# A two-layer decoder trunk: order of TensorE work around four hand-overs, and the memory norm one group earlier

## The chip, the cores and the metric

The kernel runs on one core of a Trainium2 chip. The metric is the device time of one execution in microseconds (us). Before the change it is 2344.69 us, the median of 3 runs (2342.08 to 2345.27). The core's engines are TensorE (PE: matrix multiplications and transposes, PEld its weight loads), VectorE (DVE), ScalarE (ACT), GpSimd (POOL) and SyncE (SP), whose queue issues the loads. Each engine works through its own instructions in a fixed order.

## What is computed

The reference runs a residual stream `x` of 256 rows by 2048 columns through two layers, in float32.

```python
mem_h = rms_norm(mem, mem_norm)
for i in range(DEPTH):                      # 2 layers
    h = rms_norm(x, attn_norm[i])
    if i % N_MIXERS == 0:                   # layer 0: differential attention, 16 heads, causal
        x = x + diff_attention(h, ...)
    else:                                   # layer 1: latent attention, 16 heads, causal
        x = x + mla_attention(h, ...)
    x = x + memory_cross_attention(rms_norm(x, cross_norm[i]), mem_h, ...)   # 4 heads, 256 memory rows
    x = x + sq_relu_mlp(rms_norm(x, mlp_norm[i]), ...)                       # 2048 -> 8192 -> 2048
return rms_norm(x, final_norm)
```

In the latent attention the queries come from a normed 512-wide latent row `c_q`, the keys and values from another, `c_kv`. Each head's query has a part of 128 columns and a rotated part of 64; the rotated key is shared by all heads.

## The kernel before

**Precision.** Every product is made of three passes over rounded halves: an operand is cast to a high part on ACT (`hi`) and the rest is subtracted on DVE (`lo`), and PE sums hi x hi, hi x lo and lo x hi.

**Weights.** `plan` lists the weight pieces in the order of their use, each 512 rows by 512 columns (1 MB). `split_weights` (L84) loads one into one of 3 `raw` tiles, casts its halves on ACT (L98) and subtracts on DVE (L99) into `whi` and `wlo` (4 buffers of half a piece each). `take` (L114) keeps three pieces traced ahead. All loads go through one queue, SP, in the order in which the program issues them (`load`, L75).

**Activations.** They stand transposed in units of 512 columns (`unit`, 10 buffers), with `hi` and `lo` parts for both row tiles (t = 0 and 1, 128 rows each). `matmul_chunk` (L123) multiplies a list of units with the next weight pieces into two PSUM banks, one for each row tile: for each unit 24 matmuls (4 slices of 128 rows, 2 row tiles, 3 passes). The banks come from a pool of four (`ps_mm`, tag `mm`, L53); a second pool of four (`ps_ax`) serves the attention's scores and outputs. `heads_T` (L270) takes a bank on to the next unit: ACT copies it out with a scale (`evacuate`, L250, into one of 3 `ev` tiles), PE transposes four blocks back into the same bank (`transpose4`, L184), and ACT and DVE split it (`split`, L172, lines 176 and 177). Only then is the bank free.

**Residual.** `Stream.feed` (L233) does this for a chunk of the residual when the next norm's input is made: `add_residual` (L247, DVE) adds the bank to `x`, PE transposes the new columns into the same bank, DVE scales them by the norm's gains into a tile `xg` (2 buffers, L181), the split follows, and ACT sums the squares (L205). The row scale itself is applied after the next multiplication.

**Attention.** Both attentions go in four groups of four heads (`attention`, L592). `project(gi)` makes a group's queries, keys and values; `attend(gi)` its softmax and outputs; `project_group` multiplies the group's output `o` into the residual. In program order a turn `gi` holds `attend(gi)`, the output product of group `gi - 1`, `project(gi + 1)` and `mid(gi)`. In the last turn the output product also lays out the transposed memory (`given_unit(memT, c, G_MEM)`, L190, four units, each of which takes a `raw` tile); `mem_keys` follows and then the last group's output product. `mem_norm` (L539), called by `mid`, loads the memory's rows in eight pieces of 256 KB into tiles of the tag `xg` (`memrow`, L543) and sums their squares on ACT.

**Latent group.** `project_latent` (L743) multiplies the rotated queries first into two banks `pr` (L745); POOL rotates them (`rope`, L255, six operations for each row tile, after an ACT copy). The other queries follow (L751, `heads_T` L753), then the keys' chunk (L754), the transposes of the rotated queries back into `pr` (L757) with their split, the keys' `heads_T` (L762) and the values (L763). In the first group `shared_key` (L733) also rotates the shared key, whose tiles `kr` are of the tag `xg`, copies it (L737) and transposes it (L740). The latents' own transposes are scaled into `xg` tiles as well (L707).

**Cross attention.** `attend4` (L328) weighs the memory's values in `weighted` (L359): for each head and each block of 128 memory rows three passes, and for each pair of heads a copy out of the bank (L379, L380). Its values are computed just before (`mem_values`, lines 281 and 282).

**What sets the order.** The code above gives the dependencies and, through its order, the priorities. The order on each engine is fixed when the program is built: a planner goes through the program on its own estimate of times, and on each engine takes the earliest instruction in program order that it holds to be ready (`schedule_with_timeline_sim=True`, L882). Tiles of one tag are given out in the order of their first use in the program. Loads keep program order. `tc.issue_after(ins)` adds an order without a wait: what is traced inside stands behind `ins` on its engine.

Of the kernel before, what the change touches and what calls it, by code (L numbers as in the profile page):

```python
# [17 lines left out]
P = 128  # L18
# [3 lines left out]
CH = 512  # L22
# [17 lines left out]
def trunk(ctx, tc, x, xT, mem, memT, positions, gcols, gfinal, lam_vecs, consts, W, out):  # L40
# [17 lines left out]
    def nm(s):  # L58
        serial[0] += 1
        return f"{s}_{serial[0]}"  # L60
# [48 lines left out]
            ready.append(split_weights(W[name][i, :, : 4 * width], width))  # L109

    taken = [0]
    hooks = {}

    def take():  # L114
        fill()
        got = ready.pop(0)
        fill()
        taken[0] += 1
        if taken[0] in hooks:
            hooks[taken[0]]()  # L120
        return got

    def matmul_chunk(acts, width=CH, turns=False):  # L123

        ps = [bank("mm") for _ in range(NT)]
        n = len(acts)

        def part(u, h, hi, lo, t):
            o = ps[t][:, :width]
            a = acts[u]  # L130
            for k in range(2):
                kk = 2 * h + k
# [6 lines left out]
                nc.tensor.matmul(o, ah, wh, start=first, stop=False)  # L139
                nc.tensor.matmul(o, ah, wl, start=False, stop=False)  # L140
                nc.tensor.matmul(o, al, wh, start=False, stop=last)  # L141

        for u in range(n - 2 if turns else n):
            for h, (hi, lo) in enumerate(take()):
                for t in range(NT):
                    part(u, h, hi, lo, t)
        if turns:
            parts = [(u, h, *w) for u in (n - 2, n - 1) for h, w in enumerate(take())]
            for t in range(NT):
                for p in parts:  # L150
                    part(*p, t)
        return ps
# [72 lines left out]
    class Stream:  # L225


        def __init__(self, gcol):
            self.gcol = gcol
            self.units = {}  # L230
            self.ss = [small.tile([P, 4], F32, tag="ss", name=nm("ss")) for _ in range(NT)]

        def feed(self, c, t, ps):  # L233
# [4 lines left out]
            split(self.units[c], t, scaled(pt, g[:, self.gcol + 4 * c : self.gcol + 4 * c + 4]))  # L238
            sum_squares(self.ss[t][:, c : c + 1], xc)

        def done(self):
            self.rstd = [row_norm(self.ss[t], D)[:, 0:1] for t in range(NT)]
            return [self.units[c] for c in range(4)]

    def add_residual(t, c, ps):
        xc = xs[t][:, c * CH : (c + 1) * CH]
# [37 lines left out]
    def val(v, half, kb, lo, n):  # L284
        return v[:, half, 2 * kb : 2 * kb + 2, :].rearrange("p a b -> p (a b)")[:, lo : lo + n]
# [42 lines left out]
    def attend4(score_pairs, v, dst, causal):  # L328


        pTs = [work.tile([P, 2, 2, 2, S], F32R, tag="pT", name=nm("pT")) for _ in range(2)]

        def probs(t, heads, nk):
            sb = bank()
            scores(sb, [score_pairs(h, nk) for h in heads], nk, t, causal)
            pr, rs = softmax(sb, len(heads))
            nc.vector.tensor_tensor(
                pr.rearrange("p (h k) -> p h k", k=nk), pr.rearrange("p (h k) -> p h k", k=nk),
                rs[:, : len(heads)].unsqueeze(2).broadcast_to([P, len(heads), nk]), ALU.mult,
            )  # L340
            pt = transpose4(pr, sb)
            nb = nk // P
            for p in range(heads[0] // 2, heads[-1] // 2 + 1):
                at = (2 * p - heads[0]) * nb
                src = pt[:, at : at + 2 * nb].rearrange("p (h b) q -> p h b q", b=nb)
                hi = pTs[p][:, 0, :, :nb, t * P : (t + 1) * P]
                nc.scalar.copy(hi, src)
                nc.vector.tensor_tensor(pTs[p][:, 1, :, :nb, t * P : (t + 1) * P], src, f32(hi), ALU.subtract)

        if causal:  # L350
            probs(0, range(4), P)
        for p in range(2):
            for t in range(1 if causal else 0, NT):
                probs(t, range(2 * p, 2 * p + 2), S)
        if callable(v):
            v = v()
        pos_ = [bank() for _ in range(2)]

        def weighted(p, i, kb):  # L359
            q = slice(kb * P if causal else 0, S)  # L360
            o = pos_[p][:, i * S : (i + 1) * S][:, q]
            col = (2 * p + i) * P
            mm3(
                o, val(v, 0, kb, col, P), val(v, 1, kb, col, P),
                pTs[p][:, 0, i, kb, q], pTs[p][:, 1, i, kb, q],
                kb == 0 and (causal or i == 0), kb == 1 and (causal or i == 1),
            )

        if not causal:
            for h in range(4):  # L370
                weighted(h // 2, h % 2, 0)
        for p in range(2):
            po = pos_[p]
            for i in range(2):
                for kb in (0, 1) if causal else (1,):
                    weighted(p, i, kb)
# [102 lines left out]
    acts = []  # L479
# [93 lines left out]
    def project_out(acts_o, gcol):  # L573
        nxt = Stream(gcol)
        for c in range(4):
            ps = matmul_chunk(acts_o)
            for t in range(NT):
                add_residual(t, c, ps[t])
                nxt.feed(c, t, ps[t])
        return nxt  # L580

    def project_group(o, nxt=None, each=None):
        for c in range(4):
            ps = matmul_chunk([o])
            if each:
                each(c)
            for t in range(NT):
                add_residual(t, c, ps[t])
                if nxt:
                    nxt.feed(c, t, ps[t])  # L590

    def attention(project, attend, mid, gcol):  # L592

# [29 lines left out]
    def mlp(l, norm, gnext):  # L623
        a = norm.done()
        rstd = keep2(norm.rstd, 1.0, "r1")
        hid = {}

        def up(b):
            hid[b] = []
            for c in range(2):  # L630
                dst = unit()
                ps = matmul_chunk(a)
                for t in range(NT):
                    r = work.tile([P, CH], F32, tag="ev", name=nm("ev"), bufs=3)
# [20 lines left out]
        down(7, nxt.feed)  # L655
        return nxt


# [5 lines left out]
    def project_diff(gi):  # L664
# [15 lines left out]
    norm, m, mk = attention(  # L680
        project_diff,
        lambda h, o: attend_diff(*h, o, coef, gsub),
        lambda gi: mem_norm() if gi == 2 else None,
        G_CROSS,
    )
    norm = cross(0, norm, m, mk)
# [56 lines left out]
    def project_latent(gi):  # L743
        qr, q, k, v = half_unit(), unit(), unit(), unit()
        pr = matmul_chunk([cq], 256)  # L745
        turned = []
        for t in range(NT):
            e = evacuate(pr[t][:, :256], rq[t])
            rope(e[:, :256].rearrange("p (h d) -> p h d", h=4), cos[:, t, hd:], sin[:, t, hd:], 4, hm)
            turned.append(e)  # L750
        ps = matmul_chunk([cq])  # L751
        for t in range(NT):
            heads_T(ps[t], t, rq[t], q)  # L753
        ps = matmul_chunk([ckv])  # L754
        for t in range(NT):
            for i in range(2):
                nc.tensor.transpose(pr[t][:, i * P : (i + 1) * P], turned[t][:, i * P : (i + 1) * P], ident)  # L757
# [135 lines left out]
```

## Time and profile before

| | us |
|---|---|
| median of 3 runs | 2344.69 (2342.08 to 2345.27) |
| the profiled execution | 2345.17 |
| its span, first to last instruction | 2343.4 |
| PE busy | 2305.9 (98%) |
| DVE, ACT, POOL busy | 1343.3, 1127.8, 186.2 |
| mean granted TensorE clock | 0.994 of full speed |
| read from HBM | 421.48 MB, 181 GB/s over the span |

A row of the timeline gives start, duration, engine, line of the kernel, operation, tiles (out<-in, with buffer numbers left out), a count, and in brackets the idle time before it and what ended that. The durations of matmuls overlap, since they are pipelined: the distance of two starts is what one costs. A row of waits gives the waiting engine and line, what it waited for, the total, the number of waits and the longest. A row of the chain of waits gives start, duration and what the chain passed through. A row of stretches gives the stretch, its length, the busy time and instructions of PE, PEld, DVE, ACT and POOL, the granted TensorE clock, the share of the DMA engines and GB/s.

### The profile page before, as it was taken

The numbers are of one execution on the slowest core, as the hardware profiler recorded it, in microseconds if no ns is written. First come the engines' busy times: TensorE is split into PE (matmuls) and PEld (weight loads), VectorE is DVE, ScalarE is ACT, GpSimd is POOL, SyncE is SP. The second block draws the span as 40 slices with busy tenths as digits, with TensorE's granted clock in tenths as the row PEclk, the third lists the DMA queues.
The fourth block names the chain that finished last, engine by engine and source line by source line (L and its number), as shares of the span: only waits on it lengthen the run. The fifth ranks groups of instructions, "written<-read, shape, count | busy, mean of one in ns | idle before, by whom it ended". The sixth has DMA issues, their size and how long they took to land.

```text
span 2343.4 us, 27471 instructions
## 1 busy us (share of the span) xinstructions
PE 2305.9 (98%) x10860; PEld 1922.8 (82%) x10860; DVE 1343.3 (57%) x1566; ACT 1127.8 (48%) x1539; POOL 186.2 (8%) x258
## 2 busy tenths in 40 slices
PE   8999999999999999999999999999999999999998
PEld 6888887888888888888889788888888888888886
DVE  5565657675545555555566666777455555554554
ACT  6544446554444444444445555555444444444444
POOL 1111010000000000000000211000100000000001
PEclk9999999999999999999999999999999999999999
DMA  7545556545555555555555343544555555555554
GB/s 277 173 170 171 173 187 208 178 141 184 191 186 197 181 196 184 193 185 193 185 178 179 131 136 135 198 162 162 180 195 182 198 181 195 187 190 183 195 188 153
DMA packets 64354, 425.37 MB, mean 182 GB/s; under 512 B 7392, under 2 KB 7520, under 8 KB 15328
## 3 DMA queue, kind: packets, MB, share of 16 engines
q1 hardware_dynamic: 64224, 423.61, 53.1%
q8 instruction: 85, 1.39, 0.2%
q14 instruction: 45, 0.37, 0.0%
HBM read 421.48 MB, written 2.10 MB: 181 GB/s over the span
## 4 chain that ended last, share of the span: by engine, by line
PE 94%; DMA 2%; ACT 1%; DVE 1%; POOL 1%; issue 1%; SPq 0%; ACTq 0%; POOLq 0%
PE mm L140 29%; PE mm L139 29%; PE mm L141 29%; PE mm L187 3%; PE ax L157 1%; PE ax L155 1%; PE ax L156 1%; DVE wlo L99 1%; DMA raw<-in_da_wqkv_dram 1%; ACT whi L98 1%; DMA raw<-in_ca_wkv_dram 1%; DMA memrow<-in_mem_dram 0%; PE ax L187 0%; DMA x<-in_x_dram 0%; ACT junk L205 0%
## 5 line engine op out<-in xcount | busy, mean ns | idle before, releaser
L99 DVE TENSOR_TENSOR wlo<-raw,whi 128x1024 fp32r<-128x1024 f32 (+2 forms) x794 | 960.5, 1211 | 848.7 <-ACT whi L98 846.3
L98 ACT CAST whi<-raw 128x1024 fp32r<-128x1024 f32 (+2 forms) x794 | 823.9, 1039 | 947.9 <-PE mm L141 900.8
L139 PE MATMUL mm<-whi,unit 128*128 128x512 f32 (+2 forms) x3168 | 1228.3, 389 | 7.8 <-ACT whi L98 5.3
L140 PE MATMUL mm<-wlo,unit 128*128 128x512 f32 (+2 forms) x3168 | 1230.8, 389 | 1.9 <-DVE wlo L99 1.9
L141 PE MATMUL mm<-whi,unit 128*128 128x512 f32 (+2 forms) x3168 | 1231.0, 390 | 0.0
L139 PEld LDWEIGHTS mm<-whi,unit 128*128 128x128 f32 x3168 | 596.9, 189 | 125.5 <-ACT whi L98 7.2
L140 PEld LDWEIGHTS mm<-wlo,unit 128*128 128x128 f32 x3168 | 596.9, 188 | 122.0 <-DVE wlo L99 4.4
L141 PEld LDWEIGHTS mm<-whi,unit 128*128 128x128 f32 x3168 | 596.8, 188 | 115.4
L636 POOL TENSOR_TENSOR ev<-ev 128x512 f32<-128x512 f32 x64 | 81.3, 1271 | 1163.6 <-ACT ev L635 1162.3
L247 DVE TENSOR_TENSOR x<-x,mm 128x512 f32<-128x512 f32 x208 | 135.5, 680 | 14.0 <-PE mm L141 13.5
L176 ACT CAST unit<-mm 128x512 fp32r<-128x512 f32 x104 | 61.0, 587 | 94.7 <-PE mm L187 94.6
L177 DVE TENSOR_TENSOR unit<-mm,unit 128x512 fp32r<-128x512 f32 x104 | 71.2, 687 | 53.7 <-ACT unit L176 53.7
L211 POOL TENSOR_TENSOR rs<-rs,mhalf 128x1 f32<-128x1 f32 (+1 forms) x28 | 19.5, 695 | 669.8 <-DVE rs L210 633.0
L187 PE MATMUL mm<-const,ev 128*128 128x128 f32 x416 | 62.3, 272 | 0.0
L187 PEld LDWEIGHTS mm<-const,ev 128*128 128x128 f32 x416 | 51.3, 140 | 12.3 <-ACT ev L252 0.2
L635 ACT ACTIVATE ev<-mm,r 128x512 f32<-128x512 f32 x64 | 43.8, 685 | 11.5 <-PE mm L141 11.5
L205 ACT ACTIVATE junk<-x 128x512 bf16<-128x512 f32 x56 | 35.2, 629 | 27.1 <-DVE x L247 26.2
L295 ACT ACTIVATE p<-ax,nmax 128x256 f32<-128x256 f32 (+1 forms) x80 | 33.5, 428 | 25.7 <-DVE nmax L293 25.5
L176 ACT CAST unit<-xg 128x512 fp32r<-128x512 f32 x52 | 31.5, 619 | 19.5 <-DVE xg L181 19.5
L177 DVE TENSOR_TENSOR unit<-xg,unit 128x512 fp32r<-128x512 f32 x52 | 34.8, 684 | 0.3
L263 POOL TENSOR_TENSOR rope<-ev,cos 128x64 f32<-128x64 f32 (+1 forms) x24 | 14.5, 603 | 241.7 <-ACT ev L252 240.8
L181 DVE TENSOR_TENSOR xg<-mm,g 128x512 f32<-128x512 f32 x44 | 29.4, 683 | 6.1 <-PE mm L187 4.3
(140 smaller groups left out, 754.0 us busy)
## 6 DMA issues: line engine op xcount, KB each, us to landing
raw<-in_mlp_wup_dram SPq DMA_DIRECT2D x128, 1024.0 KB, 5.0
raw<-in_mlp_wdown_dram SPq DMA_DIRECT2D x128, 1024.0 KB, 4.9
raw<-in_da_wqkv_dram SPq DMA_DIRECT2D x47, 1024.0 KB, 4.8
raw<-in_da_wo_dram SPq DMA_DIRECT2D x16, 1024.0 KB, 4.9
raw<-in_ca_wkv_dram SPq DMA_DIRECT2D x16, 1024.0 KB, 5.0
raw<-in_mla_wo_dram SPq DMA_DIRECT2D x16, 1024.0 KB, 5.0
raw<-in_ca_wq_dram SPq DMA_DIRECT2D x8, 1024.0 KB, 5.0
raw<-in_ca_wo_dram SPq DMA_DIRECT2D x8, 1024.0 KB, 4.9
```

What stands on the lines that cost most here:

```text
L98: nc.scalar.copy(hi, r)
L99: nc.vector.tensor_tensor(lo, r, f32(hi), ALU.subtract)
L139: nc.tensor.matmul(o, ah, wh, start=first, stop=False)
L140: nc.tensor.matmul(o, ah, wl, start=False, stop=False)
L141: nc.tensor.matmul(o, al, wh, start=False, stop=last)
L176: nc.scalar.copy(hi, src)
L177: nc.vector.tensor_tensor(dst[:, 1, :n, t * P : (t + 1) * P], src, f32(hi), ALU.subtract)
L187: nc.tensor.transpose(pt[:, k * P : (k + 1) * P], src[:, k * P : (k + 1) * P], ident)
L205: nc.scalar.activation(junk[:, : src.shape[1]], src, AF.Square, accum_out=acc)
L247: nc.vector.tensor_tensor(xc, xc, ps, ALU.add)
L635: nc.scalar.activation(r, ps[t], AF.Relu, scale=rstd[t])
L636: nc.gpsimd.tensor_tensor(r, r, r, ALU.mult)
```

## The change

Four edits:

1. **Rotated queries.** The four transposes of L757 are put behind the last matmul of the keys' chunk on PE (`behind(latest[0])`; `latest` holds the matmul that `matmul_chunk` traced last).
2. **Last residual chunk.** Where a norm's input is made, the fourth chunk (c == 3) is held: `hold` sums the squares at once, and `last_unit`, called by the next `matmul_chunk` ahead of its second unit, traces the transposes, the scaling and the split behind the last matmul of the first unit. This is so at five places: the output products that end both attentions and both cross attentions, and the last down product of the first MLP.
3. **Cross attention.** The order of the value passes: the passes of the second memory block that use the values' `hi` part go first for all four heads, and those that use the `lo` part last.
4. **Memory norm.** `mem_norm` is called in turn 1 in place of turn 2, behind the projection of the third group.

```diff
+    latest = [None]
+    def behind(mm):
+        return tc.issue_after(mm.ins)
...
-                nc.tensor.matmul(o, al, wh, start=False, stop=last)
+                latest[0] = nc.tensor.matmul(o, al, wh, start=False, stop=last)
         for u in range(n - 2 if turns else n):
+            if u == 1 and callable(acts[-1]):
+                acts[-1] = acts[-1]()
...
+        def hold(self, c, t, ps):
+            sum_squares(self.ss[t][:, c : c + 1], xs[t][:, c * CH : (c + 1) * CH])
+            self.held.append((c, t, ps))
+        def last_unit(self):
+            after = latest[0]
+            for c, t, ps in self.held:
+                with behind(after):
+                    pt = transpose4(xs[t][:, c * CH : (c + 1) * CH], ps)
+                if c not in self.units:
+                    self.units[c] = unit()
+                split(self.units[c], t, scaled(pt, g[:, self.gcol + 4 * c : self.gcol + 4 * c + 4]))
+            self.held = []
+            return self.units[c]
         def done(self):
-            return [self.units[c] for c in range(4)]
+            return [self.units[c] if c in self.units else self.last_unit for c in range(4)]
...
-        def weighted(p, i, kb):
+        def weighted(p, i, kb, passes, first, last):
-            mm3(...)
+            for j, (sv, sp) in enumerate(passes):
+                nc.tensor.matmul(
+                    o, val(v, sv, kb, (2 * p + i) * P, P), pTs[p][:, sp, i, kb, q],
+                    start=first and j == 0, stop=last and j == len(passes) - 1,
+                )
+        PASSES = ((0, 0), (0, 1), (1, 0))
         if not causal:
-            for h in range(4):
-                weighted(h // 2, h % 2, 0)
+            for kb, passes in ((0, PASSES), (1, PASSES[:2]), (1, PASSES[2:])):
+                for p in range(2):
+                    for i in range(2):
+                        weighted(p, i, kb, passes, kb == 0 and i == 0, passes == PASSES[2:] and i == 1)
...
-                nxt.feed(c, t, ps[t])
+                (nxt.hold if c == 3 else nxt.feed)(c, t, ps[t])
...
-        lambda gi: mem_norm() if gi == 2 else None,
+        lambda gi: mem_norm() if gi == 1 else None,
...
         ps = matmul_chunk([ckv])
         for t in range(NT):
-            for i in range(2):
-                nc.tensor.transpose(pr[t][:, i * P : (i + 1) * P], turned[t][:, i * P : (i + 1) * P], ident)
+            with behind(latest[0]):
+                for i in range(2):
+                    nc.tensor.transpose(pr[t][:, i * P : (i + 1) * P], turned[t][:, i * P : (i + 1) * P], ident)
```

More of the change, by code (lines that the diff above doesn't have):

```diff
@@ L239, in feed @@
             sum_squares(self.ss[t][:, c : c + 1], xc)
+        def hold(self, c, t, ps):
[9 more added lines that the diff above has]
+                split(self.units[c], t, scaled(pt, g[:, self.gcol + 4 * c : self.gcol + 4 * c + 4]))
+            self.held = []
+            return self.units[c]
         def done(self):
             self.rstd = [row_norm(self.ss[t], D)[:, 0:1] for t in range(NT)]
-            return [self.units[c] for c in range(4)]
+            return [self.units[c] if c in self.units else self.last_unit for c in range(4)]
     def add_residual(t, c, ps):
@@ L357, in attend4 @@
         pos_ = [bank() for _ in range(2)]
-        def weighted(p, i, kb):
+        def weighted(p, i, kb, passes, first, last):
             q = slice(kb * P if causal else 0, S)
             o = pos_[p][:, i * S : (i + 1) * S][:, q]
[L362 to L367, printed above, removed]
+            for j, (sv, sp) in enumerate(passes):
[4 more added lines that the diff above has]
+        PASSES = ((0, 0), (0, 1), (1, 0))
         if not causal:
-            for h in range(4):
-                weighted(h // 2, h % 2, 0)
+            for kb, passes in ((0, PASSES), (1, PASSES[:2]), (1, PASSES[2:])):
+                for p in range(2):
+                    for i in range(2):
+                        weighted(p, i, kb, passes, kb == 0 and i == 0, passes == PASSES[2:] and i == 1)
         for p in range(2):
             po = pos_[p]
-            for i in range(2):
-                for kb in (0, 1) if causal else (1,):
-                    weighted(p, i, kb)
+            if causal:
+                for i in range(2):
+                    for kb in range(2):
+                        weighted(p, i, kb, PASSES, kb == 0, kb == 1)
             hi = dst[:, 0, 2 * p : 2 * p + 2, :]
@@ L589, in project_group @@
                 if nxt:
-                    nxt.feed(c, t, ps[t])
+                    (nxt.hold if c == 3 else nxt.feed)(c, t, ps[t])
     def attention(project, attend, mid, gcol):
@@ L654, in mlp @@
         nxt = Stream(gnext)
-        down(7, nxt.feed)
+        down(7, lambda c, t, ps: (nxt.hold if c == 3 else nxt.feed)(c, t, ps))
         return nxt
@@ L755, in project_latent @@
         for t in range(NT):
-            for i in range(2):
-                nc.tensor.transpose(pr[t][:, i * P : (i + 1) * P], turned[t][:, i * P : (i + 1) * P], ident)
+            with behind(latest[0]):
+                for i in range(2):
+                    nc.tensor.transpose(pr[t][:, i * P : (i + 1) * P], turned[t][:, i * P : (i + 1) * P], ident)
             split(qr, t, pr[t][:, : 2 * P].rearrange("p (k t) -> p k t", k=2))
```

## The prediction

> **What bounds the kernel.** I read the page first, then PE's waits, and then the timeline around each wait.
>
> ```profile
> span 2343.4 us, 27471 instructions
> PE 2305.9 (98%) x10860; PEld 1922.8 (82%) x10860; DVE 1343.3 (57%) x1566; ACT 1127.8 (48%) x1539; POOL 186.2 (8%) x258
> ...
> L177 DVE TENSOR_TENSOR unit<-mm,unit 128x512 fp32r<-128x512 f32 x104 | 71.2, 687 | 53.7 <-ACT unit L176 53.7
> ```
>
> PE is busy for 98% of the span, and the change neither adds nor removes a matmul. So it can only fill or open gaps, of which 2343.4 - 2305.9 = 37.5 us exist, the start and the end of the kernel among them. A matmul costs the distance of two starts, not its printed duration, and that distance grows where the granted clock is low. The gaps by cause, from PE's waits:
>
> ```profile
> PE mm L757 <- POOL ev L268: 9.6, 3, 4.4
> PE ax L155 <- ACT pT L308: 3.1, 1, 3.1
> PE mm L187 <- DVE x L247: 1.3, 2, 0.7
> ```
>
> The first row is edit 1's object, the second turns out to be edit 4's, the third is what edit 2 seems to aim at. Stretches behind or in such waits show a second price:
>
> ```profile
> 1293.70:1298.20 4.50, 4.45 (x11) 3.52 (x12) 0.42 (x2) 0.00 (x0) 3.51 (x15) 0.51 0.22 93
> 1388.30:1391.00 2.70, 0.12 (x2) 0.08 (x2) 2.23 (x3) 1.77 (x4) 2.49 (x4) 1.00 0.10 39
> 1448.00:1452.50 4.50, 4.50 (x16) 3.56 (x14) 1.11 (x2) 0.89 (x2) 0.00 (x0) 0.62 0.55 215
> ```
>
> After the first latent group's wait the clock is 0.51 for 4.5 us, which loses 4.5 x 0.49 = 2.2 us; after the fourth's it is 0.62, a loss of 4.5 x 0.38 = 1.7 us; in the third's the clock stays at 1.00.
>
> **Edit 1, first latent group: a loss.** PE and its neighbours there:
>
> ```profile
> 1287.15 0.60 PE L187 MATMUL mm<-const,lat 128*128 128x128 f32 x4
> 1292.14 0.69 PE L757 MATMUL mm<-const,ev 128*128 128x128 f32 x2 [4.40 <-POOL ev L268]
> 1293.75 0.79 PE L139 MATMUL mm<-whi,unit 128*128 128x512 f32 x1 [0.92 <-DVE half L177]
> ...
> 1299.99 0.50 PE L139 MATMUL mm<-whi,unit 128*128 128x512 f32 x1
> 1294.23 0.45 POOL L268 TENSOR_TENSOR ev<-rope,rope 128x128 f32<-128x128 f32 x1
> 1296.10 0.23 DVE L737 COPY kr<-kr 128x64 f32<-128x64 f32 x1 [2.40 <-POOL kr L268]
> 1299.24 1.29 DVE L181 TENSOR_TENSOR xg<-mm,g 128x512 f32<-128x512 f32 x2 [1.57 <-PE ax L740]
> ```
>
> The queries' chunk starts at 1293.75 not when the transposes end but when the split of `half` has emptied its bank: at that moment two of the four `mm` banks hold `pr`, and two hold the second latent, whose scaling (L181) waits for an `xg` tile that the shared key keeps until its transposes at L740. So the queries' first row tile takes `pr`'s bank, and its second starts at 1299.99, behind the scaling. In the changed program `pr` isn't free until the keys' chunk is through, and the keys need the queries' banks. The queries must wait for the shared key: its copy ends at 1296.10 + 0.23, its two transposes take about 0.7 (as L757's after its wait), half of the row at 1299.24 is 0.65, so 1297.7, or 1298.4 if the second row tile's copy goes first; I take 1298.0. At 1299.99 twelve matmuls of the queries had been done. Their distance at full clock is 0.23:
>
> ```profile
> 1387.74 0.60 PE L187 MATMUL mm<-const,ev 128*128 128x128 f32 x4
> 1390.92 0.44 PE L757 MATMUL mm<-const,ev 128*128 128x128 f32 x2 [2.58 <-POOL ev L268]
> ...
> 1391.55 0.47 PE L139 MATMUL mm<-whi,unit 128*128 128x512 f32 x1
> 1391.86 0.39 PE L140 MATMUL mm<-wlo,unit 128*128 128x512 f32 x1
> 1392.09 0.40 PE L141 MATMUL mm<-whi,unit 128*128 128x512 f32 x1
> 1388.64 0.68 ACT L252 ACTIVATE ev<-mm,rq 128x512 f32<-128x512 f32 x1
> ...
> 1389.48 0.60 ACT L176 CAST unit<-mm 128x512 fp32r<-128x512 f32 x1
> 1391.39 0.37 ACT L176 CAST half<-mm 128x256 fp32r<-128x256 f32 x1 [1.32 <-PE mm L757]
> ```
>
> From 1298.0 these twelve take 12 x 0.23 = 2.8 and the low clock's 2.2, so the same work is left at 1303.0 as was at 1299.99: 3.0 us lost. The keys then wait for the queries' bank: copy 0.68, four transposes 0.4 (the six between 1390.92 and 1391.55 take 0.63), cast 0.60, subtraction 0.69 (the 687 ns above), 2.4 in all, less six matmuls of the other row tile (1.4): 1.0. The four moved transposes still cost 0.5, later. Sum: 4.5 us lost. Ends: 2.7 (start at 1297.7, no waits) and 7.5 (start at 1298.4, the whole 2.4, and 1.2 for the values, which wait for a bank too: 0.4 + 0.37 + 0.4). Below nothing lies only the case that the banks don't bind, a rival.
>
> **Edit 1, the other groups: a gain.** In the third group PE stood still for 2.58 us with the keys' chunk queued behind L757. Without L757 ahead, the queries' transposes move up by 0.2 from 1387.74 and end at 1387.9; ACT is free at 1388.64 (so its row), casts until 1389.2, DVE subtracts until 1389.9, and the second row tile's transposes (0.4) stand in between: the keys start at about 1390.3 in place of 1391.55, 1.25 earlier. The moved transposes take 0.5 of it back: 0.7 gained. What is late next is the queries' bank, through the one `ev` tile that the two unrotated copies must now share, since the two rotated ones keep theirs. The fourth group is alike (9.6 - 4.4 - 2.6 leaves it 2.6 of the row of waits), and as its gap shrinks from 2.6 to about 1.8 I count its 1.7 of low clock as gained: 2.4. In the second group nothing waited (attention of the first covered it), and the values now wait for a bank for some 0.3. Sum of the three: 2.8 gained; ends 0 and 6.9 (the two waits of 2.6 and the 1.7). Edit 1 together: 1.7 us lost.
>
> On the clock the Trainium skill, TensorE: Matmul & The Clock Gate, "What's actually happening", says that the array falls to half clock after an idle window of about 3.4 us, and that the window runs free. By it a gap of 1.8 us would not fall, which is my count; by the rows alone, where one of two gaps of 2.6 us did, half of the 1.7 could stay, and the sum would be 0.9 higher. Against the edit speaks PSUM — Partial Sum Buffer, "Summary: rules for kernel authors", with "Evacuate promptly": two of four banks are kept full over a whole chunk. By that rule the first group loses, as summed; without it the sum would be that of the first rival.
>
> **Edit 4: a gain.** The chain of waits runs through the memory's rows:
>
> ```profile
> 345.51 5.27 DMA memrow<-in_mem_dram
> ...
> 365.27 7.08 DMA raw<-in_ca_wkv_dram
> ...
> 376.51 5.06 DMA raw<-in_ca_wkv_dram
> 345.51 16.73 SPq L76 DMA_DIRECT2D memrow<-in_mem_dram  x8
> 383.96 0.58 PE L155 MATMUL ax<-unit,pT 128*128 128x256 f32 x1 [3.10 <-ACT pT L308]
> 386.16 0.73 PE L139 MATMUL mm<-whi,unit 128*128 128x512 f32 x1
> 355.00:378.80 23.80, 23.80 (x114) 19.67 (x114) 16.92 (x33) 14.54 (x37) 1.81 (x3) 1.00 0.59 192
> 378.80:394.00 15.20, 11.08 (x45) 9.29 (x45) 12.36 (x27) 9.16 (x21) 0.00 (x0) 0.78 0.53 186
> ```
>
> Eight small loads keep SP's queue for 16.7 us, each waiting for one of two `xg` tiles. The weights behind them come late; ACT waits for one of them with the attention's casts queued behind, and PE, busy without a gap until 378.8, then idles 4.1 us of 15.2 at a mean clock of 0.78. The memory keys, whose first matmul is at 386.16, need the laid-out memory, and that comes after the attention's first output split on ACT. The same split in the group before, which has no memory rows, against each group's first output matmul:
>
> ```profile
> 258.51 0.45 PE L139 MATMUL mm<-whi,unit 128*128 128x512 f32 x1
> 354.99 0.45 PE L139 MATMUL mm<-whi,unit 128*128 128x512 f32 x1
> 284.22 0.62 ACT L176 CAST unit<-xg 128x512 fp32r<-128x512 f32 x1 [0.57 <-DVE xg L181]
> 383.81 0.62 ACT L176 CAST unit<-xg 128x512 fp32r<-128x512 f32 x1
> ```
>
> That is 25.7 us against 28.8: 3.1 us earlier without the rows. I add 1.0 of the low clock's 3.3 (15.2 x 0.22), as the gap is then about 1 us: 4.0 gained in round numbers. Ends: nothing, because the memory's layout still keeps two of three `raw` tiles and the second load of `ca_wkv` (376.51) can't be issued before the first is cast; and 7.4, the idle time and the low clock together. At the new place the eight loads block SP for the same 16.7 us, ACT takes eight sums, POOL two small powers. What hides them is the weights' lead: in the old place it carried PE without a gap up to 378.8 (the stretch above), and behind the new place stand 12 plain pieces in place of the memory's layout. Price nothing; if the lead fails, 3.1, the wait seen here behind a late weight.
>
> **Edits 2 and 3: nothing.** Edit 2 moves eight transposes at each of five places behind 24 matmuls; the split, the scaling and PSUM's banks get time, as the unit is needed two units later.
>
> ```profile
> 504.81 1.47 PE L187 MATMUL mm<-const,x 128*128 128x128 f32 x12
> 506.96 0.65 PE L187 MATMUL mm<-const,x 128*128 128x128 f32 x4 [0.68 <-DVE x L247]
> 491.88 0.39 PE L157 MATMUL ax<-pT,unit 128*128 128x256 f32 x1 [0.47 <-DVE unit L282]
> 491.74 0.68 DVE L348 TENSOR_TENSOR pT<-ax,pT 128x512 fp32r<-128x512 f32 x1
> ```
>
> The waits for `x` stand behind sixteen transposes in a row, those of the first two chunks of a cross attention's output, which the edit leaves alone. It is covered by other work already, so nothing; ends a gain of 1.3 (the row of waits) and a loss of 0.7 (one such wait, if a bank comes late). Edit 3 takes away the wait for the values' `lo` at 491.88 (0.47, twice in the kernel), but the same DVE makes the second pair's probabilities next, until 492.42, and the last passes need those: nothing, between a gain of 0.9 and a loss of 1.2 (the first pair's copy out, a cast of 0.6, twice no longer beside the second pair's passes).
>
> **Sum.** The profiled execution took 2345.17, of which 1.8 lie outside its span. 2345.2 + 1.7 - 4.0 = 2342.9. It stands 0.5 above the median of the runs, so the forecast is 2342.5: a little faster, within what a measurement can tell from no change (0.2%, 4.7 us).
>
> **Rivals.** *The order pays in full.* If the banks don't bind in the first group, its 4.4 + 0.9 of waiting and 2.2 of low clock go, with 2.8 elsewhere and the memory's 4.0: 14.3 less, 2330.5. For it speaks the largest wait of the table; against it the wait for `half` at 1293.75. *The banks bind everywhere, and it ends slower.* The place is the keys' chunk in each latent group: the first loses 7.5, the second gets a gap like the third's (2.6) with the clock's 1.7, the third gets the clock's 1.7, the fourth stays: 13.5 lost, 4.0 gained, 2354. It decides from where edit 1 costs more than edit 4's 4.0. For it speaks the single `ev` tile that is left; against it that the keys' first tile needs only one bank. *The memory's wait stays*, because ACT still has the cast of `ca_wkv` queued ahead of the split: 2344.7 + 1.7 - 0.4 = 2346.0. For it speaks that this load isn't issued earlier; against it the 3.1 us between the two groups.
>
> **Chances.** Forecast 0.40 (its own range 2338 to 2346; faster 0.13, same 0.27), paid in full 0.16 (faster), banks 0.20 (slower 0.18, same 0.02), memory's wait stays 0.24 (same 0.16, slower 0.07, faster 0.01). Faster 0.30, same 0.45, slower 0.25. The range from 2331 to 2353 leaves about half of the two outer cases outside, 2 in 10.
>
> **What would show it.** L757 no longer in PE's waits, and in its place in the first latent group a wait of some 10 us ahead of the queries' chunk, for DVE's scaling or L740; the chunk of keys in the third group about 1 us earlier; no low clock in the fourth; the memory keys' first matmul some 3 us earlier against the group's first output matmul, and no gap behind the new place of the rows. Wrong makes it above all a planner that orders ACT or PE differently at these places, since it goes by its own estimates.

## The result and the profile after

The changed kernel takes 2353.09 us (median of 7 runs, 2349.06 to 2354.25), the kernel before, on the same chip, 2344.12 (2342.08 to 2345.46). The ratio is 1.0034, interval 1.0023 to 1.0046: about 9 us slower. The forecast was 2342.5.

From the page and from PE's waits of the changed kernel (engine, line waited for, total, times, longest; L145 to L147 are now the three passes, L195 `transpose4`, L184 and L185 the split, L189 the scaling, L272 `add_residual`, L277 `evacuate`, L293 the last of a rotation's six operations, L786 the rotated queries' transposes, L768 the shared key's, L333 the attention's cast):

```profile
span 2351.3 us, 27448 instructions
PE 2306.4 (98%) x10860; PEld 1921.4 (82%) x10860; DVE 1344.3 (57%) x1566; ACT 1128.4 (48%) x1539; POOL 186.2 (8%) x258
```

```profile
PE ax L768 <- POOL kr L293: 9.0, 2, 8.4
PE mm L195 <- ACT ev L277: 8.7, 6, 1.8
PE mm L195 <- DVE x L272: 1.4, 2, 0.7
PE ax L163 <- ACT pT L333: 0.5, 1, 0.5
```

PE's work is the same (2306.4 against 2305.9), and the span is 7.9 longer, so gaps grew. The wait of 9.6 for the rotated queries is gone. Two rows have come in its place: 9.0 for the shared key, and six waits of up to 1.8, 8.7 together, for the copy of an unrotated row tile. The wait of 3.1 for the attention's cast has become 0.5.

Where the time went can be counted. For two neighbouring matmuls I take the distance of their starts less the median distance of that shape in the same execution, and add this up over a place; waits and low clock both show in it. The last column is the difference of the medians, each against the kernel before on the same chip. In us, for every kernel of this study:

| kernel | latent group 1 | 2 | 3 | 4 | sum | memory keys and rows | median against before |
|---|---|---|---|---|---|---|---|
| before | 8.5 | 0.7 | 2.9 | 4.5 | 16.5 | 7.3 | |
| after | 17.5 | 2.8 | 4.3 | 4.3 | 28.8 | 3.4 | +9.0 |
| plain place of the rotated queries | 7.5 | 0.7 | 2.9 | 4.4 | 15.5 | 3.0 | -3.3 |
| rotated queries moved, alone | 14.7 | 2.8 | 4.3 | 5.8 | 27.6 | 5.6 | +12.9 |
| memory's norm moved, alone | 8.0 | 0.7 | 2.9 | 4.5 | 16.1 | 2.4 | -3.1 |
| rows apart | 14.8 | 2.4 | 5.9 | 4.3 | 27.3 | 4.7 | +8.5 |
| new bank | 10.2 | 0.9 | 2.4 | 2.4 | 16.0 | 4.6 | -5.9 |
| new bank, rows apart | 10.0 | 1.5 | 1.0 | 1.0 | 13.4 | 3.1 | -7.8 |
| key apart | 9.7 | 2.8 | 4.2 | 4.3 | 21.0 | 2.1 | +0.3 |
| new bank, rows and key apart | 2.4 | 1.5 | 1.0 | 1.0 | 5.8 | 2.7 | -15.5 |
| plain place, rows and key apart | 6.2 | 0.7 | 4.5 | 4.5 | 15.9 | 2.4 | -4.5 |

The changed kernel lost 12.3 in the latent groups and won 3.9 at the memory. Each row is one execution, and a low clock falls in one place or another, so a column differs by up to 3 without a cause in the edit (17.5 and 14.7 in the first group of the changed kernel and of the one with that move alone).

The first latent group of the changed kernel, PE and then ACT and DVE from the timeline (here and below, rows between are left out):

```profile
1282.42 0.60 PE L195 MATMUL mm<-const,lat 128*128 128x128 f32 x4
1291.37 0.73 PE L768 MATMUL ax<-const,kr 128*128 128x128 f32 x2 [8.35 <-POOL kr L293]
...
1293.45 0.63 PE L145 MATMUL mm<-whi,unit 128*128 128x512 f32 x1
1298.38 0.47 PE L145 MATMUL mm<-whi,unit 128*128 128x512 f32 x1
1301.24 0.60 PE L195 MATMUL mm<-const,ev 128*128 128x128 f32 x4
1303.61 0.66 PE L195 MATMUL mm<-const,ev 128*128 128x128 f32 x4 [1.77 <-ACT ev L277]
1304.40 0.50 PE L145 MATMUL mm<-whi,unit 128*128 128x512 f32 x1
1313.49 0.50 PE L145 MATMUL mm<-whi,unit 128*128 128x512 f32 x1 [0.90 <-DVE half L185]
```

```profile
1301.44 1.04 ACT L98 CAST whi<-raw 128x1024 fp32r<-128x1024 f32 x1 [0.34 <-PE mm L147]
1302.39 0.58 ACT L184 CAST unit<-mm 128x512 fp32r<-128x512 f32 x1
1292.14 0.69 DVE L189 TENSOR_TENSOR xg<-mm,g 128x512 f32<-128x512 f32 x1 [0.57 <-PE ax L768]
1302.52 1.22 DVE L99 TENSOR_TENSOR wlo<-raw,whi 128x1024 fp32r<-128x1024 f32 x1 [0.16 <-ACT whi L98]
1303.66 0.68 DVE L185 TENSOR_TENSOR unit<-mm,unit 128x512 fp32r<-128x512 f32 x1
```

The queries' chunk starts at 1293.45, eleven us after the latent's transposes, once the shared key is transposed and the scaling (L189) has emptied a bank. It runs at low clock. The twelve matmuls of its second row tile start at 1298.38, and only behind them PE transposes the first row tile (1301.24). Its cast and subtraction (L184, L185) stand behind the next weights' split (L98, L99), so its bank is free at 1303.66 + 0.68. The keys' chunk waits for that, to 1304.40, and then the values' to 1313.49. The third group, PE, ACT and DVE:

```profile
1394.29 0.60 PE L195 MATMUL mm<-const,ev 128*128 128x128 f32 x4
1396.66 0.66 PE L195 MATMUL mm<-const,ev 128*128 128x128 f32 x4 [1.77 <-ACT ev L277]
1397.60 0.50 PE L145 MATMUL mm<-whi,unit 128*128 128x512 f32 x1 [0.28 <-DVE unit L185]
1394.49 1.04 ACT L98 CAST whi<-raw 128x1024 fp32r<-128x1024 f32 x1 [0.45 <-PE mm L147]
1395.44 0.58 ACT L184 CAST unit<-mm 128x512 fp32r<-128x512 f32 x1
1395.57 1.38 DVE L99 TENSOR_TENSOR wlo<-raw,whi 128x1024 fp32r<-128x1024 f32 x1 [1.68 <-ACT whi L98]
1396.87 0.68 DVE L185 TENSOR_TENSOR unit<-mm,unit 128x512 fp32r<-128x512 f32 x1
```

The keys need the bank that the queries' first row tile leaves. On ACT and DVE the split of the next weights (L98 1.04, L99 1.38) stands ahead of that bank's split, so the bank is free at 1396.87 + 0.68, and the keys start 3.3 after the transposes of 1394.29. The granted clock by stretch (PE, PEld, DVE, ACT, POOL busy, then clock, DMA share, GB/s):

```profile
1394.20:1397.50 3.30, 1.35 (x10) 0.81 (x8) 1.93 (x2) 2.26 (x4) 3.22 (x7) 1.00 0.32 134
1397.50:1401.20 3.70, 3.60 (x16) 2.99 (x17) 0.74 (x2) 0.93 (x2) 0.17 (x1) 1.00 0.88 283
1291.30:1297.90 6.60, 5.89 (x15) 4.47 (x16) 3.09 (x6) 1.24 (x2) 1.31 (x7) 0.50 0.01 2
1301.20:1304.40 3.20, 1.30 (x10) 0.79 (x8) 2.98 (x3) 2.21 (x4) 0.00 (x0) 1.00 0.00 0
1304.40:1308.00 3.60, 3.60 (x10) 2.80 (x11) 0.69 (x1) 0.49 (x1) 0.00 (x0) 0.57 0.88 289
```

In the first group the clock is low twice, 0.50 behind the long wait and 0.57 behind the keys' wait; in the third group, after a wait of the same kind, it stays at 1.00.

At the memory, the first output matmul of the group and the first of the memory's keys, and the stretches behind the rows' new place:

```profile
355.29 0.45 PE L145 MATMUL mm<-whi,unit 128*128 128x512 f32 x1
382.21 0.40 PE L145 MATMUL mm<-whi,unit 128*128 128x512 f32 x1
250.00:274.00 24.00, 24.00 (x114) 19.95 (x113) 13.48 (x25) 13.89 (x33) 1.12 (x2) 1.00 0.67 228
274.00:278.00 4.00, 3.82 (x24) 3.07 (x23) 3.97 (x5) 3.60 (x6) 0.00 (x0) 1.00 0.58 201
379.00:397.00 18.00, 16.33 (x80) 12.98 (x79) 13.56 (x27) 12.50 (x27) 0.00 (x0) 1.00 0.61 213
```

These keys start 26.9 after the group's first output matmul, against 31.2 before; the clock, 0.78 there before, is 1.00. PE has no gap at the rows' new place up to 274, and in this execution it loses some 0.6 just behind it. In the eight other kernels with the rows at the new place nothing is lost there: the same count from 240 to 300 gives 0.3 to 0.4, as before the change.

### The profile page after: what moved, and what is told of

Same layout as the page of the kernel before. It is cut to its first block, busy times and chain, and to the rows that moved or that the text cites. A ratio compares the mean times of both kernels' runs of the same rounds, so it can differ in the third digit from the quotient of the medians.

```text
span 2351.3 us, 27448 instructions
## 1 busy us (share of the span) xinstructions
PE 2306.4 (98%) x10860; PEld 1921.4 (82%) x10860; DVE 1344.3 (57%) x1566; ACT 1128.4 (48%) x1539; POOL 186.2 (8%) x258
## 4 chain that ended last, share of the span: by engine, by line
PE 93%; DMA 2%; ACT 2%; DVE 2%; issue 1%; POOL 0%; SPq 0%; ACTq 0%; POOLq 0%
PE mm L145 29%; PE mm L146 29%; PE mm L147 29%; PE mm L195 2%; ACT whi L98 1%; DVE wlo L99 1%; PE ax L163 1%; PE ax L165 1%; DMA raw<-in_da_wqkv_dram 1%; PE ax L164 1%; PE ax L388 1%; PE ax L195 0%; DMA memrow<-in_mem_dram 0%; DMA x<-in_x_dram 0%; ACT junk L213 0%
## 5 line engine op out<-in xcount | busy, mean ns | idle before, releaser
L99 DVE TENSOR_TENSOR wlo<-raw,whi 128x1024 fp32r<-128x1024 f32 (+2 forms) x794 | 961.0, 1212 | 854.0 <-ACT whi L98 852.0
L98 ACT CAST whi<-raw 128x1024 fp32r<-128x1024 f32 (+2 forms) x794 | 823.7, 1039 | 946.4 <-PE mm L147 903.7
L145 PE MATMUL mm<-whi,unit 128*128 128x512 f32 (+2 forms) x3168 | 1227.9, 389 | 9.4 <-ACT whi L98 6.4
L147 PE MATMUL mm<-whi,unit 128*128 128x512 f32 (+2 forms) x3168 | 1230.3, 390 | 0.0
L145 PEld LDWEIGHTS mm<-whi,unit 128*128 128x128 f32 x3168 | 596.6, 188 | 128.0 <-ACT whi L98 8.4
L147 PEld LDWEIGHTS mm<-whi,unit 128*128 128x128 f32 x3168 | 596.5, 188 | 116.0 <-DVE unit L207 0.2
L272 DVE TENSOR_TENSOR x<-x,mm 128x512 f32<-128x512 f32 x208 | 135.9, 681 | 15.2 <-PE mm L147 14.7
L184 ACT CAST unit<-mm 128x512 fp32r<-128x512 f32 x104 | 61.0, 587 | 91.3 <-PE mm L195 91.3
L185 DVE TENSOR_TENSOR unit<-mm,unit 128x512 fp32r<-128x512 f32 x104 | 71.0, 687 | 49.5 <-ACT unit L184 49.4
L195 PE MATMUL mm<-const,ev 128*128 128x128 f32 x416 | 62.7, 273 | 8.7 <-ACT ev L277 8.7
L195 PEld LDWEIGHTS mm<-const,ev 128*128 128x128 f32 x416 | 50.7, 140 | 21.5 <-ACT ev L277 10.1
L184 ACT CAST unit<-xg 128x512 fp32r<-128x512 f32 x52 | 31.3, 618 | 27.5 <-DVE xg L189 27.5
L185 DVE TENSOR_TENSOR unit<-xg,unit 128x512 fp32r<-128x512 f32 x52 | 34.5, 686 | 1.9 <-ACT unit L184 1.6
L288 POOL TENSOR_TENSOR rope<-ev,cos 128x64 f32<-128x64 f32 (+1 forms) x24 | 14.7, 611 | 251.2 <-ACT ev L277 250.3
L189 DVE TENSOR_TENSOR xg<-mm,g 128x512 f32<-128x512 f32 x44 | 29.1, 684 | 5.1 <-PE mm L195 4.3
```

Of the source, the lines that this page charges most:

```text
L98: nc.scalar.copy(hi, r)
L99: nc.vector.tensor_tensor(lo, r, f32(hi), ALU.subtract)
L147: latest[0] = nc.tensor.matmul(o, al, wh, start=False, stop=last)
L185: nc.vector.tensor_tensor(dst[:, 1, :n, t * P : (t + 1) * P], src, f32(hi), ALU.subtract)
L195: nc.tensor.transpose(pt[:, k * P : (k + 1) * P], src[:, k * P : (k + 1) * P], ident)
L272: nc.vector.tensor_tensor(xc, xc, ps, ALU.add)
```

## The experiments

**Which edit makes the loss.** Three kernels. The first takes the rotated queries' order back:

```diff
-            with behind(latest[0]):
-                for i in range(2):
-                    nc.tensor.transpose(pr[t][:, i * P : (i + 1) * P], turned[t][:, i * P : (i + 1) * P], ident)
+            for i in range(2):
+                nc.tensor.transpose(pr[t][:, i * P : (i + 1) * P], turned[t][:, i * P : (i + 1) * P], ident)
```

> The changed kernel with the rotated queries' transposes back where they stood before; the residual's last transposes, the values' order and the memory's norm stay changed. Theory (the rotated queries' move makes the whole loss, 12.3 us by the distances from matmul to matmul, and the memory's norm gives back 4.6 less 0.7): about 2340, 4 below the kernel before; PE's waits for the shared key's and the queries' transposes as before (first latent group 8.5 over its plain length, where the changed kernel has 17.5). Rival (the loss comes from the residual's or the values' edit, or from an order of the rest that the planner chose anew): 2348 or more.

The second is the kernel before with this order alone (the diff reversed, with `latest` and `behind`):

> The kernel before with nothing but the rotated queries' transposes put behind the keys' chunk. Theory: all the loss and none of the memory's gain, 12.3 above the kernel before, 2356. Rival (the loss needs the other edits beside it): 2344 to 2350, with PE's six waits of 1.8 for the queries' and keys' copies not there.

The third is the kernel before with the memory's norm moved alone:

```diff
-        lambda gi: mem_norm() if gi == 2 else None,
+        lambda gi: mem_norm() if gi == 1 else None,
```

> The kernel before with nothing but the memory's norm in the turn of the second group. Theory (the memory's rows were what the memory's keys waited for; 7.3 over the plain length there falls to 2.7, and 0.7 is paid at the rows' new place): 2340.2, 3.9 below the kernel before, and within 1 of the kernel that has the residual's and the values' edits as well. Rival (the gain at the memory's keys comes from elsewhere, or the rows' new place costs what the old one did): 2344.

Measured: 2339.72 (ratio 0.9986, 0.9977 to 0.9995), 2355.98 (1.0051, 1.0038 to 1.0063) and 2340.00 (0.9987, 0.9978 to 0.9996), with the kernel before at 2343.05. From the waits of the first and of the second (their L785 is the rotated queries' transposes; L746 the shared key's, L193 `transpose4`, L258 `evacuate`):

```profile
PE mm L785 <- POOL ev L293: 9.6, 3, 4.4
```

```profile
PE ax L746 <- POOL kr L274: 9.0, 2, 8.4
PE mm L193 <- ACT ev L258: 8.7, 6, 1.8
```

All three came out as the theory had them. The rotated queries' move makes the whole loss, 12 to 13 by the medians (9.0 + 3.3 and 12.9), and brings both new rows of waits with it. The memory's norm alone is worth 3.1, and the residual's and the values' edits beside it nothing that can be told (2339.7 against 2340.0).

**Row buffer or bank.** The wait names an `ev` tile: of three, two hold the rotated rows until the transposes. Here these rows get other buffers, which lie idle in this layer:

```diff
-            e = evacuate(pr[t][:, :256], rq[t])
+            e = work.tile([P, S], F32, tag="a", name=nm("a"))
+            nc.scalar.activation(e, pr[t][:, :256], AF.Copy, scale=rq[t])
```

> The changed kernel, with the rotated queries' rows in buffers of their own size that lie idle in this layer (those of the first attention's combined probabilities), so that the three row buffers serve the unrotated queries and the keys alone; the matmul banks are held as in the changed kernel. Theory A (the one row buffer left makes the waits): PE's row of six waits of 1.8 (8.7 us together) for the copy into that buffer goes, and about 8 of the loss with it: 2345. Theory B (the banks make them): the keys' first matmul still waits for both queries' banks to be copied out, the wait only changes its name (to the copies out of the turned queries' bank), and no more than 3 is won: 2350 to 2353.

Measured: 2351.57 (1.0038, 1.0025 to 1.0050), which is 8.5 above the kernel before, where the changed kernel is 9.0 above: no gain that can be told. The third group, PE, ACT and DVE, and its clock:

```profile
1391.46 0.60 PE L195 MATMUL mm<-const,ev 128*128 128x128 f32 x4
1393.34 0.66 PE L195 MATMUL mm<-const,ev 128*128 128x128 f32 x4 [1.29 <-ACT ev L277]
1394.77 0.50 PE L145 MATMUL mm<-whi,unit 128*128 128x512 f32 x1 [0.77 <-DVE unit L185]
1392.73 1.38 DVE L99 TENSOR_TENSOR wlo<-raw,whi 128x1024 fp32r<-128x1024 f32 x1 [1.68 <-ACT whi L98]
1394.03 1.31 DVE L185 TENSOR_TENSOR unit<-mm,unit 128x512 fp32r<-128x512 f32 x2
```

```profile
1391.40:1394.70 3.30, 1.31 (x9) 0.78 (x8) 1.97 (x3) 2.70 (x4) 3.22 (x6) 1.00 0.32 134
1394.70:1398.40 3.70, 3.63 (x9) 2.90 (x10) 0.64 (x2) 0.00 (x0) 0.14 (x1) 0.56 0.82 283
```

The second copy comes earlier, but the keys start 3.3 after the first transposes as before: DVE's weight split ends at 1394.11, and the queries' bank is split only then. The row buffer isn't what binds. PE's row of waits for the copies only fell from 8.7 to 6.9, since ACT's queue still sets when a copy is made (at 1392.61, behind a weight cast of 1391.66), and the release that sets the keys' start is the bank's.

**The bank.** Now the rotated queries' banks come free with their copy, because the transposes, at the same place, go into one newly taken bank:

```diff
         ps = matmul_chunk([ckv])
+        both = bank("mm")
         for t in range(NT):
+            pt = both[:, t * S : (t + 1) * S]
             with behind(latest[0]):
                 for i in range(2):
-                    nc.tensor.transpose(pr[t][:, i * P : (i + 1) * P], turned[t][:, i * P : (i + 1) * P], ident)
-            split(qr, t, pr[t][:, : 2 * P].rearrange("p (k t) -> p k t", k=2))
+                    nc.tensor.transpose(pt[:, i * P : (i + 1) * P], turned[t][:, i * P : (i + 1) * P], ident)
+            split(qr, t, pt[:, : 2 * P].rearrange("p (k t) -> p k t", k=2))
```

> The changed kernel, but the rotated queries' transposes, still behind the keys' chunk, go into one newly taken matmul bank, so that their chunk's two banks come free when their rows are copied out; the rows stay in the row buffers. Theory B (the held banks make the waits): the keys' chunk starts without the wait of 2.55 in the third and fourth latent groups, the first group loses its second stretch of low clock and wait (3.99 there), and the values' 1.71 in three groups falls under 0.7: 3.99 + 2 x 2.55 + 3 x 1.0 = 12.1 won, 2341. Theory A2 (bank and row buffer both bind, either alone holds it): no more than 3 won, 2350 or more, and the gain only comes with the rows apart as well. The first group's wait of 8.59 for the shared key stays by both.

And with the rows apart as well:

> The newly taken bank and the rows in buffers of their own together. Theory B: within 2 of the kernel with the new bank alone (2341), since the row buffers' wait then lies behind the keys' chunk. Theory A2: 2341 here, and 8 or more below the kernel with the new bank alone.

Measured: 2337.51 (0.9976, 0.9968 to 0.9985) and 2335.57 (0.9968, 0.9956 to 0.9979), with before at 2343.38. The new bank alone turns 9.0 lost into 5.9 won, some 15, and more than the 12.1 expected. The expectation let the first group's wait for the shared key stay at 8.59; it is 4.4 now, because the first group's queries no longer wait for the latent's banks either. From its waits:

```profile
PE ax L768 <- POOL kr L293: 4.4, 1, 4.4
PE mm L195 <- ACT ev L277: 3.3, 3, 1.5
```

The row buffer is next in line: three waits of 3.3 together are left for it, they go when the rows stand apart, and the third and fourth group fall from 2.4 to 1.0. That was within the 2 that were expected, and the intervals of the two kernels overlap. So the bank bound first and the buffer second: the bank hid the buffer's price, which was 0.5 alone and 1.9 behind the new bank, by the medians.

**The shared key.** Its tiles leave the two `xg` buffers:

```diff
-        e = work.tile([P, 4, P], F32, tag="xg", name=nm("kr"))
+        e = work.tile([P, 4, P], F32, tag="pT", name=nm("kr"), padded_shape=[P, 16, P])
```

> The changed kernel, with the shared key's two row tiles in buffers that lie idle there (those of the transposed probabilities) instead of the two that the scaling after a transposition uses. Theory (in the first latent group the queries' chunk waits for the banks of the latent's transposes, these for the scaling, and the scaling for the shared key's tiles, which come free only after its rotation and transposes): the wait of 8.59 falls to at most 3 and the low clock behind it (2.2 to 2.8) goes, 8 to 9 won, 2344 to 2345, and the shared key's transposes are no longer ahead of the queries' chunk. Rival (GpSimd's rotations set that wait anyway, by the rotated queries' rows): 2 won at the most, 2351 or more.

Measured: 2343.71 (1.0005, 0.9996 to 1.0014), 0.3 above the kernel before where the changed kernel is 9.0 above: 8.7 won. The first group:

```profile
1281.54 0.50 PE L145 MATMUL mm<-whi,unit 128*128 128x512 f32 x1
1287.12 0.60 PE L195 MATMUL mm<-const,ev 128*128 128x128 f32 x4
1293.27 0.47 PE L768 MATMUL ax<-const,kr 128*128 128x128 f32 x1 [5.55 <-POOL kr L293]
```

The size was right, the way only half: the queries' chunk now starts with no wait (1281.54), which shows that the key's tiles held it. But the wait is not gone: the key's transposes, now behind that chunk, wait 5.55 for GpSimd's rotations, and behind them the clock is low again (0.50 from 1294.2 to 1298.2). The rival was right that much.

**All three.**

> The changed kernel with the new bank, the rows apart and the shared key apart. Theory (the two causes lie at different places and add up): 12 and 8.5 below the changed kernel, 2332 to 2334, which is about what the order was worth by the prediction's rival of full pay (2330.5). Rival (the one wait uncovers the other, or the next one, GpSimd's rotation): 2340 or more.

Measured: 2327.93 (0.9938, 0.9925 to 0.9950), 15.5 below the kernel before and faster than both kernels. Against the changed kernel that is 24.5 won, and the parts add up: 16.8 with the new bank and the rows apart (9.0 + 7.8), 8.7 with the key apart. The 2332 to 2334 expected took 12 for the first part, where it is 16.8; above all, the new bank brought the first latent group from 17.5 to 10.2, where 3.99 had been expected. PE there:

```profile
1282.44 0.48 PE L145 MATMUL mm<-whi,unit 128*128 128x512 f32 x1
...
1294.35 0.57 PE L768 MATMUL ax<-const,kr 128*128 128x128 f32 x2
1295.72 0.56 PE L768 MATMUL ax<-const,kr 128*128 128x128 f32 x2 [0.79 <-POOL kr L293]
1296.78 0.38 PE L789 MATMUL mm<-const,a 128*128 128x128 f32 x2
1297.74 0.50 PE L145 MATMUL mm<-whi,unit 128*128 128x512 f32 x1 [0.58 <-DVE unit L185]
```

The queries' and the keys' chunks run from 1282.44 to 1294.35 without a wait, and only then the shared key and the rotated queries (L789) follow; 0.79 of the 9.0 is left. Whether the explicit order is still needed once the bank is taken late wasn't measured.

**Is it the place, or the buffers?** The plain place of the transposes with both buffer changes, beside the fastest version again:

> The kernel with the plain place of the rotated queries' transposes (ahead of the keys' chunk, into their own banks), with the rows and the shared key in buffers of their own as in the fastest version, but without the newly taken bank. Theory (what the fastest version wins over the plain order is the place of the transposes, which the new bank makes free of charge): TensorE's three waits for GpSimd's rotation ahead of the transposes, 9.6 together in the plain order, stay for the most part, 2336 to 2340. Rival (the row buffers and the key's tiles alone win it, the place of the transposes nothing): 2330 or less.

> The version with the new bank, the rows and the shared key apart, beside the one without the new bank on the same chip: 2328 to 2330, 6 to 10 below it by the theory, within 2 of it by the rival.

Measured: 2338.20 (0.9979, 0.9971 to 0.9988) and 2329.40 (0.9944, 0.9930 to 0.9957), with before at 2342.69. From the waits of the first:

```profile
PE mm L786 <- POOL a L293: 9.1, 3, 4.0
```

The late place with its new bank is worth 8.8, and the fastest version stands 13.3 below the kernel before this time; the buffers alone leave GpSimd's wait where it was, 9.1 after 9.6.

## Why the prediction was wrong

**Edit 1, first group: 4.5 forecast, 9.0 measured.** The mechanism and the first half were right to 0.2. Set by the latent's transposes (1287.15 before, 1282.42 after, 4.73 apart), the queries started at 1298.2 (forecast 1298.0), and twelve of their matmuls were done at 1303.1 (forecast 1303.0). The step that failed is the next one, "the keys then wait for the queries' bank", sized at 1.0. It cost 4.0 in the table's measure: 2.4 of wait and 1.6 of a second low clock, and the values 1.2 that I had kept for the upper end. Two things were wrong in the sizing. I set six matmuls of the other row tile against the chain of copy, transposes, cast and subtraction; there are twelve, but PE takes them ahead of the transposes, which start 2.0 after their copy has ended (1298.55 + 0.69), so they hide the copy alone. And I had summed the steps as if ACT and DVE were free for them; the next weights' split stands ahead, 1.04 on ACT and 1.22 on DVE in this group, so that the bank comes free 3.1 after the transposes start, where the durations of transposes, cast and subtraction make 1.7. This is read from the order of the queues; no run took the weight split away.

The second low clock is one execution's: with this move alone the same stretch of the first group, PE busy for 1.31 in 3.20, is followed by a clock of 1.00, and so is the keys' wait there with the rows apart. (The lower end of the first group's loss, 2.7, also left out the 0.5 of the moved transposes that the sum and the upper end hold.)

**Edit 1, the other groups: 2.8 gained forecast, 3.3 lost measured.** The same sizing failed: the third group's keys were to start 1.25 earlier, and started only 0.5 earlier, 3.3 instead of 3.8 after the first transposes. The prediction let DVE subtract from 1389.2 to 1389.9, and in the kernel before a weight split holds DVE there until 1390.14:

```profile
1388.77 1.37 DVE L99 TENSOR_TENSOR wlo<-raw,whi 128x1024 fp32r<-128x1024 f32 x1 [1.68 <-ACT whi L98]
```

The values' wait, sized at 0.3 and in the second group alone, was 1.7 in each of three groups, since the `pr` banks come free behind four moved transposes, a cast and a subtraction with another weight split among them. Group by group: second 0.3 lost forecast, 2.1 measured; third 0.7 gained, 1.4 lost; fourth 2.4 gained, 0.2 measured. Its low clock did go, as counted, but by luck: with the move alone it is there (0.54 from 1454.6 to 1458.2). Behind the keys' wait the clock fell once in each of three kernels: in the first group of the changed one, in the fourth with the move alone, in the third with the rows apart.

**Which limit.** I had the queries' bank come late through the one `ev` tile that is left, and the row of waits names that tile's copy too; the runs showed that the bank is held up by the queues without it, and that the tile comes behind.

**Edit 4: 4.0 gained forecast; 3.9 in the trace of the changed kernel, 3.1 when made alone.** The memory's keys came 4.3 earlier against the group's first output matmul, where some 3 had been forecast, and the attention's wait fell from 3.1 to 0.5. The price of the new place, nothing, held in every kernel but the changed one, whose profiled execution lost some 0.6 there.

**Edits 2 and 3: nothing forecast, nothing that can be told measured** (both together, 2339.7 against 2340.0). The waits for `x` are 1.4 after 1.3. For edit 3 the reason was wrong: the wait for the values' `lo` was to go, and it stays, 1.0 in two waits after 0.9 (`PE ax L388 <- DVE unit L307: 1.0, 2, 0.5`).

**The rivals.** *The banks bind everywhere* came true: 13.5 lost and 4.0 gained forecast, 12.3 and 3.9 measured, 2354 against 2353.1. That the sum is so near is in part luck: its parts were 7.5, 4.3, 1.7 and 0 by group, and 9.0, 2.1, 1.4 and -0.2 were measured. I had spoken against it with the keys' first row tile needing only one bank, and it is just that bank which comes late. *The order pays in full*, 2330.5, is about what the version with bank, rows and key apart reaches (2328 to 2329). *The memory's wait stays* did not come: the wait fell to 0.5.

## What to carry over

When an instruction is moved behind a long chunk, list what it keeps: its bank and its source buffer stay taken for the whole chunk, and the next two chunks queue for the rest. A chain of evacuations must be priced in the order of PE's, ACT's and DVE's queues, with the matmuls and weight splits that stand among its steps, not as a sum of durations. Taking a new destination late and copying out early gave the moved work its gain without the hold; a limit by one resource is only told from the next by relieving each alone and both together.

## What the runs showed of the hardware

A wait broken by a few short transposes can lower the clock, and the same one need not. At the keys' chunk, PE was busy for 1.30 us in a stretch of 3.20 in the first group of the changed kernel, with no idle time longer than 1.77 in it, and the clock then was 0.57. In the first group of the kernel with that move alone it was busy for 1.31 in 3.20, and the clock stayed at 1.00. In the third group of the changed kernel it was busy for 1.35 in 3.30, and the clock stayed at 1.00; with the rows apart, at the same place, 1.31 in 3.30, with no idle time longer than 1.29, and 0.56. The Trainium skill (TensorE: Matmul & The Clock Gate, "What's actually happening") gives a window of about 3.4 us that runs free, which agrees with the outcome changing for one and the same gap. I took from it that a gap of 1.8 would not lower the clock, and the first and the last of these four stretches show that it can when short pieces of work and idle time alternate.
